# Column sums of the first FFN's modulation vectors: from matmuls against ones to trees of accumulating DMAs

## The chip, the cores and the metric

The kernel runs on one core of one Trainium2 chip. The metric is device time in microseconds. A core has five engines that matter here, each with its own instruction stream in a fixed order: TensorE (PE: matmuls; PEld is its weight load), VectorE (DVE), ScalarE (ACT), GpSimd (POOL) and SyncE (SP). SP here only issues DMAs; GpSimd can issue DMAs too. An engine starts its next instruction when the one before is done with it and the semaphores that it waits for have come. Matmul results land in PSUM, in banks of 128 partitions by 512 fp32 columns; all else lies in SBUF, with 128 partitions.

## The reference

Two layers over 256 latent tokens (and, in layer 0, 256 context tokens) of width 1024. Each layer is an FFN, a mixer (attention in layer 0, a short convolution in layer 1) and an FFN again. Every sub-layer is modulated by nine vectors, made from a conditioning vector:

```
m  = (silu(c)     @ ada_w[i] + ada_b[i]).reshape(BATCH, 9, 1, D)   # latent
mc = (silu(c_ctx) @ ada_w[i] + ada_b[i]).reshape(9, D)             # context
def half_step_ffn(x, shift, scale, gate, w_in, w_out, g, b):
    y = swiglu_ffn(x * (1 + scale) + shift, w_in, w_out)           # (silu(a) * u) @ w_out
    return layer_norm(DN_ALPHA * x + 0.5 * gate * y, g, b)
x   = half_step_ffn(x,   m[:, 0], m[:, 1], m[:, 2], ...)
ctx = half_step_ffn(ctx, mc[0],   mc[1],   mc[2],   ...)
hx, hc = x * (1 + m[:, 4]) + m[:, 3], ctx * (1 + mc[4]) + mc[3]    # into attention
```

`D` is 1024, the FFN's inner width 2816. `ada_w` is 1024 x 9216 per layer. The vectors are matrix-vector products: little arithmetic, much weight traffic, and a sum over all 1024 rows.

## The kernel before

**Matmuls and weight units.** A fp32 product is made from two halves: ScalarE copies a weight tile into a rounded high half (L216, for activations L118), VectorE subtracts it to make the low half (L219, L119), and TensorE adds up high x high, high x low and low x high. The step on VectorE is called a split here, L219 for weights. A weight unit is one load by SP (`w1r`, `w2r`, `wqr`), two high and two low pieces (`w1h`, `w1l` and so on). The raw tiles rotate through 4 buffers, the high and the low ones through 5 each (`WB`). In the first FFN every sixth unit takes its halves from one extra pair (`whx`, `wlx`, `ext[0] = 1`), so there are six in all.

**The first FFN** takes latent and context tokens together: four tiles of 128 tokens, 512 columns. It runs in three parts (`fh`), with 4, 4 and 3 panels of inner columns. In a part, TensorE multiplies the panels (`f`, L725), ScalarE and VectorE form silu(a)·u (VectorE's products are L735) and split it (`gh`, `gl`). Then the part's share of `w_out` follows, bank after bank: first half of the width (n = 0) for the four token tiles, then the second; each bank takes 24 matmuls in the first two parts. When a bank is done, VectorE does the residual: L415 multiplies it by the gate (`res`), L420 or L418 adds it to the token tile (`x`, `xc`). In the last part the layer norm follows: BN_STATS (L422), the aggregate (L429), two small operations on GpSimd for the standard deviation (`rs`, L431 and L432), the normalisation (L442), then transposes and modulated activations `hT` (ScalarE's high, VectorE's low half), and the attention's query product with four weight units (`wqr`, `wqh`, `wql`; TensorE's tile `wq`).

**The background stream** makes the modulation vectors of this stage beside the FFN. It is a generator, `ada`; the FFN's code calls `tick()` after each pair of matmul groups, and the stream goes one step further when its rate (0.45 and 0.44 steps per tick) has added up to one. A step loads 128 rows of one vector's columns (`ar`, 512 KB, SP, 3 buffers). VectorE multiplies them by the conditioning vector's entries and adds them into an accumulator of 128 partitions x 1024 (`acc`, 2 buffers): L302 for the first of eight loads, L304 multiply-add for the others, each in two halves of 512. After eight loads an accumulator is whole, but each partition still holds its own part of the sum. The seven groups of the stage, two vectors each, 14 in all:

```
set_background(stream([(0, 2, 0), (0, 2, 1)], [(0, 3, 0), (0, 3, 1)], [(0, 4, 0), (0, 4, 1)],
                      [(0, 5, 0), (0, 6, 0)], [(0, 7, 0), (0, 8, 0)], [(1, 0, 0), (1, 1, 0)],
                      [(1, 2, 0), (1, 3, 0)]), 0.45)
```

The triples are layer, vector, and 0 for latent or 1 for context. The first three groups share one weight load between the two vectors; the last four hold two different vectors, each of them loaded for itself. The first group is the gate of the first FFN itself, the second and third are shift and scale for attention.

**The end of a group.** Two fp32 matmuls per vector against a 128 x 32 tile of ones sum the partitions (L339, bank `ada`); VectorE adds the bias rows (`adab`, loaded by SP), and SP writes the result to `scr`, a DRAM tile with a row for each vector. From there it is read back where it is needed: the gate broadcast to all partitions (SP, L789, after the first part's panels), and shift and scale as rows for a transpose (`fold_cols`, tile `mrow`, L389) ahead of the last part's output product. Those 28 matmuls stand in TensorE's queue among the FFN's.

In later stages vectors are summed another way (`on_pool`): GpSimd's own reduction over the partitions (`red`, L353), and an accumulating DMA from GpSimd's queue into `scr` (L354).

**What sets the order.** TensorE's order is that of the code. On the other engines a scheduler orders instructions by priority and by when it reckons their operands are there; code in a `high_priority` block goes ahead or, with a negative offset, behind. A tile's buffers are reused in order: the first writer of a new tile waits for the last reader of the one that had the buffer.

Of the kernel before, what the change touches and what calls it, by code (L numbers as in the profile page):

```python
# [18 lines left out]
P = 128  # L19
D = 1024  # L20
# [55 lines left out]
def backbone_kernel(  # L76
# [20 lines left out]
    last_split, last_lo = [], []  # L97
    ext = [1, 0]
    ada_late = [0]
# [141 lines left out]
    win_sb = cp.tile([P, 64], F32, tag="wmask", name="wmask")  # L241
    ones = cp.tile([P, 32], F32, tag="ones", name="ones")
    ident = cp.tile([P, P], F32, tag="ident", name="ident")
# [22 lines left out]
    nc.scalar.activation(cst[:, :, 0:2], pt[:, 0:16].rearrange("p (v k) -> p k v", v=2), AF.Silu)  # L266
    nc.vector.memset(ones, 1.0)
    sel = cp.tile([P, 4], F32, tag="sel", name="sel")
# [9 lines left out]

    bias_rows = []
    on_pool = [False]  # L280
# [3 lines left out]
    def ada(vecs):  # L284
# [4 lines left out]
        def accumulate(l, m, k, w):  # L289
            with ExitStack() as st:  # L290
                for i in gate_ins + (last_lo if on_pool[0] else []):
                    st.enter_context(tc.issue_after(i.ins))
                for i, vec in enumerate(vecs):
                    if vec[:2] != (l, m):
                        continue
                    if k == 0:
                        acc[i] = hp.tile([P, D], F32, tag="acc", bufs=2, name=nm("acc"))
                    sc = cst[:, k, vec[2]:vec[2] + 1]
                    for h in range(2):
                        src, a = (c[:, h * 512:(h + 1) * 512] for c in (w, acc[i]))  # L300
                        if k == 0:
                            nc.vector.tensor_scalar(a, src, sc, None, op0=ALU.mult)  # L302
                        else:
                            nc.vector.scalar_tensor_tensor(out=a, in0=src, scalar=sc, in1=a,  # L304
                                                           op0=ALU.mult, op1=ALU.add)
            if on_pool[0] and k == KC - 1:
                sums.extend((vec, acc[i]) for i, vec in enumerate(vecs) if vec[:2] == (l, m))

# [13 lines left out]
        if on_pool[0]:  # L322
            return
        n = 2 * len(vecs)
        if not bias_rows:
            bias_rows.append(hp.tile([P, 512], F32, tag="adab", name=nm("adab")))
            nc.gpsimd.memset(bias_rows[0], 0.0)
        bt = bias_rows[0]
        for i, (l, m, v) in enumerate(vecs):
            sync.dma_start(bt[64 * i:64 * i + 64:32], ada_b[l, m * D:(m + 1) * D].rearrange("(a b) -> a b", b=512))  # L330
        yield 1
        yield 1
        yield 1
        rows = hp.tile([P, 512], F32, tag="adar", name=nm("adar"))
        ps = tpb("ada")
        for i in range(len(vecs)):
            for h in range(2):
                j = 2 * i + h
                nc.tensor.matmul(ps[32 * j:32 * j + 32, :], ones, acc[i][:, h * 512:(h + 1) * 512], start=True, stop=True)  # L339
# [43 lines left out]

    def fold_cols(l, v, m, ln):

        r = sm.tile([32, P], F32, tag="mrow", bufs=2, name=nm("mrow"))
        for i, src in enumerate((scr[l][v, (m + 1) * D:(m + 2) * D], scr[l][v, m * D:(m + 1) * D],
                                 ln_g[ln[0], ln[1]], ln_b[ln[0], ln[1]])):
            sync.dma_start(r[8 * i:8 * i + 8], src.rearrange("(a b) -> a b", b=P))  # L389

# [202 lines left out]
    w_in, w_out = ffn_w_in[0, 0], ffn_w_out[0, 0]  # L593
    ab0 = hp.tile([P, D], F32, tag="acc", bufs=2, name="ab0")
    nc.vector.memset(ab0, 0.0)
# [151 lines left out]
    for q, (k0, n) in enumerate(steps):  # L747
        nxt = start_step(*steps[q + 1]) if q < 4 else iter(())
        for g in range(6 * n):
# [21 lines left out]
    for fh, (p0, p1) in enumerate(parts):  # L771
# [517 lines left out]
```

## Time and profile before

| what | value |
|---|---|
| time, median of 3 runs | 1247.95 us (1247.05 to 1248.7) |
| the profiled execution | 1247.93 us |
| its span in the profile | 1246.1 us |
| granted TensorE clock, mean | 0.999 |
| memory traffic | 275.67 MB, mean 221 GB/s |
| GpSimd's DMA queue (q0) | 160 packets, 0.02 MB |

How to read the profile: the busy share says how much of the span an engine worked. The chain follows the work that ended last back to what released it at each step, and says by whose work the end was set. The windows cut the span in stretches; the stage of the change runs to about 412 us. In timeline rows the columns are start in us from the span's start, duration in us, engine, line, operation and tiles (out<-in) and how many instructions the row joins; brackets give the wait ahead of it and what ended it. `PEclk` is the granted clock of TensorE. A name such as `ar<-in_ada_w_dram` is a DMA from a DRAM input into the tile `ar`.

### The profile page before, as it was taken

Reading aid. Unit: us, or ns where it says so; the run is one execution under the profiler, and the core shown is the slowest. Engines: PE = TensorE matmul, PEld = TensorE weight load, DVE = VectorE, ACT = ScalarE, POOL = GpSimd, SP = SyncE. Lnnn points to the kernel's source line nnn. Section 1 sums busy time; section 2 is a strip of 40 time slices with the busy share of each in tenths; the row PEclk is TensorE's granted clock in tenths of the full one; section 3 lists DMA queues with packets and bytes.
Section 4 is the critical chain, followed back from the end, with each engine's and each line's share of the span. In section 5 each row is a group of like instructions: output and inputs, shape, how many; then the busy total and the mean of one; then the engine's idle time right before and its main releaser. Section 6 shows DMA issues by size and latency. Waiting matters only on the chain.

```text
span 1246.1 us, 17225 instructions
## 1 busy us (share of the span) xinstructions
PE 1227.6 (99%) x5794; PEld 994.6 (80%) x5794; DVE 964.0 (77%) x1675; ACT 644.7 (52%) x1233; POOL 81.7 (7%) x90
## 2 busy tenths in 40 slices
PE   8999999999999999999999999999999999999997
PEld 5787778778778878777888888888878877888886
DVE  3698987788868867888877677878768798877646
ACT  2433132322325556587778635668635644677631
POOL 0000000000001011120000020020020110000200
PEclk9999999999999999999999999999999999999999
DMA  9976678778852654455899857889956764899741
GB/s 308 309 246 213 190 236 287 260 266 274 286 179 79 183 118 87 114 109 145 261 303 299 276 200 248 230 255 317 300 198 221 219 219 153 224 302 257 252 156 68
DMA packets 232304, 275.67 MB, mean 221 GB/s; under 512 B 59622, under 2 KB 178910, under 8 KB 232216
## 3 DMA queue, kind: packets, MB, share of 16 engines
q1 hardware_dynamic: 232020, 274.54, 73.0%
q8 instruction: 45, 0.74, 0.2%
q14 instruction: 43, 0.35, 0.1%
q0 software_dynamic: 160, 0.02, 0.1%
q10 hardware_dynamic: 36, 0.02, 0.0%
HBM read 265.27 MB, written 2.20 MB: 215 GB/s over the span
## 4 chain that ended last, share of the span: by engine, by line
PE 87%; DVE 4%; DMA 4%; ACT 2%; issue 2%; SPq 1%; POOL 0%; DVEq 0%; ACTq 0%
PE f L725 19%; PE w L170 17%; PE w L171 17%; PE w L173 17%; PE wkv L170 2%; PE wkv L171 2%; PE wkv L173 2%; DMA ar<-in_ada_w_dram 2%; PE wc L170 1%; PE wc L173 1%; PE wc L171 1%; DMA wor<-in_na_w_out_dram 1%; PE S L1020 1%; PE hT L450 1%; DMA wcr<-in_sc_w_in_dram 1%
## 5 line engine op out<-in xcount | busy, mean ns | idle before, releaser
L219 DVE TENSOR_TENSOR w1l<-w1r,w1h 128x512 fp32r<-128x512 f32 (+1 forms) x352 | 230.4, 698 | 44.2 <-ACT w1h L216 43.3
L216 ACT ACTIVATE w1h<-w1r 128x512 fp32r<-128x512 f32 (+1 forms) x352 | 198.4, 618 | 115.5 <-PE w L173 52.8
L170 PE MATMUL w<-w1h,hTh 128*128 128x512 f32 x528 | 206.2, 391 | 1.3 <-ACT hTh L118 1.3
L171 PE MATMUL w<-w1l,hTh 128*128 128x512 f32 x528 | 205.6, 389 | 0.0
L304 DVE SCALAR_TENSOR_TENSOR acc<-ar,cst,acc 128x512 f32<-128x512 f32 x266 | 186.6, 746 | 10.8 <-DMA ar<-in_ada_w_dram 10.8
L170 PE MATMUL w<-w2h,gh 128*128 128x512 f32 (+1 forms) x446 | 173.4, 389 | 0.0
L171 PE MATMUL w<-w2l,gh 128*128 128x512 f32 (+1 forms) x446 | 172.3, 387 | 1.1 <-DVE w2l L219 1.1
L216 ACT ACTIVATE w2h<-w2r 128x512 fp32r<-128x512 f32 x176 | 101.5, 624 | 135.0 <-PE w L173 102.9
L173 PE MATMUL w<-w1h,hTl 128*128 128x512 f32 x528 | 162.6, 389 | 0.0
L219 DVE TENSOR_TENSOR w2l<-w2r,w2h 128x512 fp32r<-128x512 f32 x176 | 113.9, 687 | 54.7 <-ACT w2h L216 53.3
L173 PE MATMUL w<-w2h,gl 128*128 128x512 f32 (+1 forms) x446 | 136.1, 386 | 0.0
L725 PE MATMUL f<-h0h,w1h 128*128 128x512 f32 x352 | 132.8, 393 | 1.2 <-ACT w1h L216 0.6
L725 PE MATMUL f<-h0l,w1h 128*128 128x512 f32 x352 | 133.2, 391 | 0.0
L725 PE MATMUL f<-h0h,w1l 128*128 128x512 f32 x352 | 132.7, 390 | 0.0
L170 PEld LDWEIGHTS w<-w1h,hTh 128*128 128x128 f32 x528 | 99.1, 188 | 22.5 <-ACT hTh L118 2.1
L173 PEld LDWEIGHTS w<-w1h,hTl 128*128 128x128 f32 x528 | 99.0, 188 | 21.0 <-DVE hTl L119 0.4
L171 PEld LDWEIGHTS w<-w1l,hTh 128*128 128x128 f32 x528 | 99.1, 188 | 20.6 <-DVE w1l L219 0.3
L170 PEld LDWEIGHTS w<-w2h,gh 128*128 128x128 f32 x446 | 83.8, 188 | 19.2 <-issue 1.7
L171 PEld LDWEIGHTS w<-w2l,gh 128*128 128x128 f32 x446 | 83.8, 188 | 18.3 <-DVE w2l L219 1.9
L173 PEld LDWEIGHTS w<-w2h,gl 128*128 128x128 f32 x446 | 83.3, 188 | 17.1
L725 PEld LDWEIGHTS f<-h0h,w1h 128*128 128x128 f32 x352 | 65.5, 188 | 19.6 <-issue 4.2
L725 PEld LDWEIGHTS f<-h0l,w1h 128*128 128x128 f32 x352 | 65.5, 188 | 14.4 <-issue 1.0
(195 smaller groups left out, 1765.8 us busy)
## 6 DMA issues: line engine op xcount, KB each, us to landing
w1r<-in_ffn_w_in_dram SPq DMA_DIRECT2D x340, 256.0 KB
ar<-in_ada_w_dram SPq DMA_DIRECT2D x128, 512.0 KB
w2r<-in_ffn_w_out_dram SPq DMA_DIRECT2D x88, 512.0 KB
ar<-in_ada_w_dram SPq DMA_DIRECT2D x32, 256.0 KB
wkvr<-in_na_w_qkv_dram SPq DMA_DIRECT2D x32, 256.0 KB
wcr<-in_sc_w_in_dram SPq DMA_DIRECT2D x32, 256.0 KB
wqr<-in_na_w_qkv_dram SPq DMA_DIRECT2D x8, 512.0 KB
wor<-in_na_w_out_dram SPq DMA_DIRECT2D x8, 512.0 KB
```

Of the source, the lines that this page charges most:

```text
L170: nc.tensor.matmul(ps, lh, rh, start=first and i == 0, stop=False)
L171: nc.tensor.matmul(ps, lh, rl, start=False, stop=False)
L173: nc.tensor.matmul(ps, ll, rh, start=False, stop=last and i == n - 1)
L216: last_split[:] = [nc.scalar.activation(hi[:, a:a + m // W_HI], raw[:, a:a + m // W_HI], AF.Copy)]
L219: last_lo[:] = [nc.vector.tensor_tensor(out=lo[:, a:b], in0=raw[:, a:b], in1=hi[:, a:b].bitcast(F32), op=ALU.subtract)]
L304: nc.vector.scalar_tensor_tensor(out=a, in0=src, scalar=sc, in1=a, op0=ALU.mult, op1=ALU.add)
L450: nc.tensor.transpose(ps[:, k * P:(k + 1) * P], z[h][:, k * P:(k + 1) * P], ident)
L725: nc.tensor.matmul(ps, w, hT0[k][part == 1], start=(k == part == 0), stop=(k == KC - 1 and part == 1))
L1020: nc.tensor.matmul(banks[i], (qh, qh, ql)[f][ps, qs], (kh, kl, kh)[f][ps, :], start=f == 0, stop=f == 2)
```

## The change

The ones, the bias rows, the matmuls, their eviction and SP's writes are gone. When a group's last load is accumulated, a tree halves the accumulator seven times: the DMA adds partitions n to 2n-1 onto 0 to n-1, for n = 64, 32, ... 1. An eighth accumulating DMA adds row 0 to the vector's row in `scr`, into which three DMAs from SP have put the biases ahead of the stage. All tree steps are on GpSimd's queue, as are now the gate's broadcast and the `scr` rows of `mrow`. Each step needs the one before it on the same accumulator. The accumulators are five instead of two; the extra pair of weight halves is given up for them (`ext[0] = 0`). Where the group ended with four steps of the stream, five empty ones stand now.

```diff
-    ext = [1, 0]
+    ext = [0, 0]
...
-                        acc[i] = hp.tile([P, D], F32, tag="acc", bufs=2, name=nm("acc"))
+                        acc[i] = hp.tile([P, D], F32, tag="acc", bufs=2 if on_pool[0] else 5, name=nm("acc"))
...
-            if on_pool[0] and k == KC - 1:
-                sums.extend((vec, acc[i]) for i, vec in enumerate(vecs) if vec[:2] == (l, m))
+            if k == KC - 1:
+                ready = [(vec, acc[i]) for i, vec in enumerate(vecs) if vec[:2] == (l, m)]
+                if on_pool[0]:
+                    sums.extend(ready)
+                    return
+                n = P // 2
+                while n:
+                    for _, a in ready:
+                        nc.gpsimd.dma_start(a[0:n], a[n:2 * n], accum_op=ALU.add)
+                    n //= 2
+                for (l, m, v), a in ready:
+                    nc.gpsimd.dma_start(scr[l][v:v + 1, m * D:(m + 1) * D], a[0:1], accum_op=ALU.add)
...
-        for i, (l, m, v) in enumerate(vecs):
-            sync.dma_start(bt[64 * i:64 * i + 64:32], ada_b[l, m * D:(m + 1) * D].rearrange("(a b) -> a b", b=512))
-        yield 1
-        yield 1
-        yield 1
-        rows = hp.tile([P, 512], F32, tag="adar", name=nm("adar"))
-        ps = tpb("ada")
-        for i in range(len(vecs)):
-            for h in range(2):
-                j = 2 * i + h
-                nc.tensor.matmul(ps[32 * j:32 * j + 32, :], ones, acc[i][:, h * 512:(h + 1) * 512], start=True, stop=True)
-        nc.vector.tensor_tensor(out=rows[:32 * n], in0=ps[:32 * n], in1=bt[:32 * n], op=ALU.add)
-        for i, (l, m, v) in enumerate(vecs):
-            sync.dma_start(scr[l][v, m * D:(m + 1) * D].rearrange("(a b) -> a b", b=512),
-                           rows[64 * i:64 * i + 64:32, :])
-        yield 1
+        for _ in range(5):
+            yield 1
...
-    def fold_cols(l, v, m, ln):
+    def fold_cols(l, v, m, ln, q=sync):
...
-            sync.dma_start(r[8 * i:8 * i + 8], src.rearrange("(a b) -> a b", b=P))
+            (q if i < 2 else sync).dma_start(r[8 * i:8 * i + 8], src.rearrange("(a b) -> a b", b=P))
...
+    for l, v, r in ((0, 0, slice(2 * D, 9 * D)), (0, 1, slice(2 * D, 5 * D)), (1, 0, slice(0, 9 * D))):
+        sync.dma_start(scr[l][v, r].rearrange("(a b) -> a b", a=16), ada_b[l, r].rearrange("(a b) -> a b", a=16))
     sync.dma_start(win_sb, win_mask)
...
-                sync.dma_start(big.rearrange("p a b -> p (a b)"),
+                nc.gpsimd.dma_start(big.rearrange("p a b -> p (a b)"),
...
-            GB = [fold_cols(0, v, 3, (0, 0)) for v in range(2)]
+            GB = [fold_cols(0, v, 3, (0, 0), nc.gpsimd) for v in range(2)]
...
-    sync.dma_start(scr[1][0, 4 * D:9 * D].rearrange("(a b) -> a b", a=16), ada_b[1, 4 * D:9 * D].rearrange("(a b) -> a b", a=16))
```

Three places show how the order moves; a row joins like instructions (x2), and the numbers behind the tiles' names count the tiles. In the changed kernel lines are numbered anew: L713 is the FFN's matmul that was L725, L403 the residual that was L415, L301 the multiply-add that was L304, L419 GpSimd's part of the layer norm that was L431.

**TensorE, third panel of the first part.** Before, the first group's ones matmuls stand between two weight units of the panel (`w1h_867`, then `w1h_876`):

```order
L725 MATMUL f_160_951<-h0h_449,w1l_868 128x512
L725 MATMUL f_160_951<-h0l_450,w1h_867 128x512
L339 MATMUL ada_971<-acc_711,ones 32x512 x2
L339 MATMUL ada_971<-acc_714,ones 32x512 x2
L725 MATMUL f_160_951<-h0h_545,w1h_876 128x512
L725 MATMUL f_160_951<-h0h_545,w1l_877 128x512
```

Now:

```order
L713 MATMUL f_159_964<-h0l_426,w1h_868 128x512
L713 MATMUL f_159_964<-h0h_447,w1h_868 128x512
L713 MATMUL f_159_964<-h0h_447,w1l_869 128x512
L713 MATMUL f_159_964<-h0l_448,w1h_868 128x512
L713 MATMUL f_159_964<-h0h_543,w1h_877 128x512
```

The two rows of L339 are gone and the unit's matmuls follow each other; at the other six places it is the same, and nothing else moves on TensorE.

**VectorE, the first residuals of the first part.** Before, the residual of the first token tile stands among the multiply-adds of the second group (`acc_994`, `acc_997`), ahead of the first split of the next `w_out` unit (`w2l_1311`):

```order
L304 SCALAR_TENSOR_TENSOR acc_994<-ar_1177,cst,acc_994 128x512
L415 SCALAR_TENSOR_TENSOR res_1197<-w_190_1136,gate_1124 128x512
L304 SCALAR_TENSOR_TENSOR acc_994<-ar_1177,cst,acc_994 128x512
L420 SCALAR_TENSOR_TENSOR x_122<-x_122,res_1197 128x512
L304 SCALAR_TENSOR_TENSOR acc_997<-ar_1177,cst,acc_997 128x512 x2
L304 SCALAR_TENSOR_TENSOR acc_994<-ar_1207,cst,acc_994 128x512 x2
L304 SCALAR_TENSOR_TENSOR acc_997<-ar_1207,cst,acc_997 128x512 x2
L415 SCALAR_TENSOR_TENSOR res_1233<-w_203_1200,gate_1124 128x512
L219 TENSOR_TENSOR w2l_1311<-w2r_1309,w2h_1310 128x512
L420 SCALAR_TENSOR_TENSOR x_124<-x_124,res_1233 128x512
L219 TENSOR_TENSOR w2l_1311<-w2r_1309,w2h_1310 128x512
L219 TENSOR_TENSOR w2l_1326<-w2r_1324,w2h_1325 128x512 x2
```

Now:

```order
L219 TENSOR_TENSOR w2l_1312<-w2r_1310,w2h_1311 128x512
L403 SCALAR_TENSOR_TENSOR res_1195<-w_186_1134,gate_1122 128x512
L219 TENSOR_TENSOR w2l_1312<-w2r_1310,w2h_1311 128x512
L408 SCALAR_TENSOR_TENSOR x_120<-x_120,res_1195 128x512
L299 TENSOR_SCALAR acc_1379<-ar_1377,cst 128x512 x2
L299 TENSOR_SCALAR acc_1382<-ar_1377,cst 128x512 x2
L301 SCALAR_TENSOR_TENSOR acc_1379<-ar_1397,cst,acc_1379 128x512 x2
L301 SCALAR_TENSOR_TENSOR acc_1382<-ar_1397,cst,acc_1382 128x512
L403 SCALAR_TENSOR_TENSOR res_1251<-w_199_1198,gate_1122 128x512
L301 SCALAR_TENSOR_TENSOR acc_1382<-ar_1397,cst,acc_1382 128x512
L408 SCALAR_TENSOR_TENSOR x_122<-x_122,res_1251 128x512
L301 SCALAR_TENSOR_TENSOR acc_1379<-ar_1425,cst,acc_1379 128x512 x2
```

The second group is through before the first residual, half a split stands ahead of it, and behind it come the third group's products (L299) and multiply-adds (L301): four and eleven of them stand between the first residual and the split of `w2l_1327`, the unit that follows, with two more residuals.

**GpSimd, from its first DMA, and ahead of the layer norm.** Before, no DMA of this stage is on GpSimd's queue: behind the set-up its next instruction is the layer norm's `rs`. Now the first group's tree and the gate stand first; these are the pair's last halving, the eighth step, the gate, and the start of the second group's tree:

```order
L311 DMA acc_712<-acc_712 1x16x64
L311 DMA acc_715<-acc_715 1x16x64
L314 DMA scr_114<-acc_712 16x1x64
L314 DMA scr_114<-acc_715 16x1x64
L779 DMA gate_1122<-scr_114 128x1024
L779 DMA gate_1124<-scr_114 128x1024
L311 DMA acc_1016<-acc_1016 64x1024
L311 DMA acc_1019<-acc_1019 64x1024
```

The stage's last tree and the layer norm's first operations:

```order
L311 DMA acc_3097<-acc_3097 16x1024
L311 DMA acc_3097<-acc_3097 8x1024
L311 DMA acc_3097<-acc_3097 4x1024
L311 DMA acc_3097<-acc_3097 2x1024
L311 DMA acc_3097<-acc_3097 1x16x64
L314 DMA scr_115<-acc_3097 16x1x64
L419 TENSOR_TENSOR rs_3379<-mv_3377,lnc 128x1
L420 TENSOR_TENSOR rs_3379<-rs_3379,lnc 128x1
```

Two accumulators alternate level by level in the first three groups; in the others each vector has a tree of its own, and the layer norm stands behind all 14.

More of the change, by code (lines that the diff above doesn't have):

```diff
@@ L241, in backbone_kernel @@
     win_sb = cp.tile([P, 64], F32, tag="wmask", name="wmask")
-    ones = cp.tile([P, 32], F32, tag="ones", name="ones")
     ident = cp.tile([P, P], F32, tag="ident", name="ident")
@@ L266, in backbone_kernel @@
     nc.scalar.activation(cst[:, :, 0:2], pt[:, 0:16].rearrange("p (v k) -> p k v", v=2), AF.Silu)
-    nc.vector.memset(ones, 1.0)
     sel = cp.tile([P, 4], F32, tag="sel", name="sel")
@@ L276, in backbone_kernel @@
     xscr = tc.dram_tile([2 * P, D], F32, name="xscr")
-    bias_rows = []
     on_pool = [False]
@@ L593, in backbone_kernel @@
     w_in, w_out = ffn_w_in[0, 0], ffn_w_out[0, 0]
-    ab0 = hp.tile([P, D], F32, tag="acc", bufs=2, name="ab0")
+    ab0 = hp.tile([P, D], F32, tag="acc", bufs=2 if on_pool[0] else 5, name="ab0")
     nc.vector.memset(ab0, 0.0)
```

5 lines of the change are left out of this document (removed).

## The prediction

> **What bounds the kernel now.** I read the page first: busy times, then the chain.
>
> ```profile
> span 1246.1 us, 17225 instructions
> PE 1227.6 (99%) x5794; PEld 994.6 (80%) x5794; DVE 964.0 (77%) x1675; ACT 644.7 (52%) x1233; POOL 81.7 (7%) x90
> PE 87%; DVE 4%; DMA 4%; ACT 2%; issue 2%; SPq 1%; POOL 0%; DVEq 0%; ACTq 0%
> ```
>
> TensorE is busy 99% of the span, and 87% of the chain that ended last is its own work. The table by windows shows the stage of the change:
>
> ```profile
> core 0: us, PE busy (x) PEld busy (x) DVE busy (x) ACT busy (x) POOL busy (x), PEclk, DMA share, GB/s
> 50.00:100.00 50.00, 50.00 (x225) 40.47 (x224) 43.28 (x73) 18.38 (x33) 0.00 (x0) 1.00 0.73 232
> 100.00:150.00 50.00, 50.00 (x225) 40.47 (x224) 47.75 (x77) 13.34 (x23) 0.00 (x0) 1.00 0.71 222
> 300.00:350.00 50.00, 50.00 (x225) 40.47 (x224) 41.00 (x65) 14.22 (x25) 0.00 (x0) 1.00 0.86 278
> 350.00:412.00 62.00, 62.00 (x294) 50.47 (x293) 48.23 (x91) 31.01 (x67) 3.33 (x8) 1.00 0.35 104
> ```
>
> In the first FFN, up to 412 us, TensorE never stops and its granted clock is 1.00 (the windows between read the same). So whatever leaves its queue there shortens the run, if nothing else makes it wait. VectorE is the near rival: 47.75 of 50 us between 100 and 150. GpSimd is idle until 350.
>
> **Term 1: the column sums leave TensorE.** Seven groups end in fp32 matmuls against a column of ones; the chain has them as seven pieces, first and last:
>
> ```profile
> 96.56 1.00 PE ada L339 x8
> ...
> 360.95 1.00 PE ada L339 x8
> ```
>
> A piece costs more than its 1.00, because the stream of FFN matmuls breaks and restarts. TensorE's timeline around the third piece:
>
> ```profile
> 171.83 0.39 PE L725 MATMUL f<-h0h,w1l 128*128 128x512 f32 x1
> 172.06 0.39 PE L725 MATMUL f<-h0l,w1h 128*128 128x512 f32 x1
> 172.38 1.06 PE L339 MATMUL ada<-acc,ones 128*32 128x512 f32 x8
> 173.38 0.50 PE L725 MATMUL f<-h0h,w1h 128*128 128x512 f32 x1
> ...
> 174.64 0.40 PE L725 MATMUL f<-h0l,w1h 128*128 128x512 f32 x1
> ```
>
> The FFN matmul that starts at 174.64 is the sixth behind the one at 172.06 (four lie in the gap). Undisturbed they start 0.227 us apart (171.83 to 172.06), six in 1.36; the rest of the 2.58 us, 1.22, is the piece. Seven of them: **-8.5 us** (by the chain's own 1.00 it would be -7.0, the small end of this term).
>
> VectorE also loses seven evictions of about 0.6 us, and SP some 30 small transfers. Neither is the bound, so I count nothing. A wait goes with them:
>
> ```profile
> DVE acc L302 <- PE ada L339: 6.1, 3, 2.9
> ```
>
> It cost nothing while TensorE was full. But without it, and with five accumulators, VectorE takes the multiply-adds earlier, as term 4 uses.
>
> **Term 2: when does the first gate arrive?** A tree is a chain on GpSimd: seven halvings, an accumulate into DRAM, then the gate's broadcast, each waiting for the one before. The trace of before has no SBUF-to-SBUF accumulate. The nearest rows are the five accumulates into DRAM late in the run, one of them with what VectorE did then and with SP's read that waited for it:
>
> ```profile
> L354 POOL DMA_DIRECT2D scr<-red x5: 997/997/1118, 727.3 to 1158.5; - x5
> DMA to landing us min/median/max: 2.6/3.5/4.0
> 912.27 1.28 DVE L219 TENSOR_TENSOR w2l<-w2r,w2h 128x512 fp32r<-128x512 f32 x2
> 913.01 1.00 POOL L354 DMA_DIRECT2D scr<-red  x1 [0.29 <-POOL red L353]
> 916.37 0.30 SPq L389 DMA_DIRECT2D mrow<-scr  x1
> ```
>
> From issue to the dependent issue is 913.01 to 916.37, 3.4 us; over the five a hop is 2.6 to 4.0, 1.0 of it the issue. Two accumulators per level issue in 2.0, less than a hop, so a pair costs one chain. These rows move 4 KB. The first two levels move 256 and 128 KB, and the gate 512 KB; loads of 256, 512 and 256 KB stand in the chain:
>
> ```profile
> 22.81 5.03 DMA ar<-in_ada_w_dram
> 558.60 11.95 DMA wor<-in_na_w_out_dram
> 1043.05 2.93 DMA w1r<-in_ffn_w_in_dram
> ```
>
> I take 4.5 and 4.0 for the two wide levels (estimates, between 2.93 and 5.03), 3.5 for the other six hops, and 5.0 for the gate, near the 5.03: 4.5 + 4.0 + 6 x 3.5 + 5.0 = 34.5. Where the tree starts, and who waits:
>
> ```profile
> 84.85 2.73 DVE L304 SCALAR_TENSOR_TENSOR acc<-ar,cst,acc 128x512 f32<-128x512 f32 x4
> 98.61 1.27 DVE L302 TENSOR_SCALAR acc<-ar,cst 128x512 f32<-128x512 f32 x3
> 120.94 0.69 DVE L415 SCALAR_TENSOR_TENSOR res<-w,gate 128x512 f32<-128x512 f32 x1
> 122.81 4.06 DVE L304 SCALAR_TENSOR_TENSOR acc<-ar,cst,acc 128x512 f32<-128x512 f32 x6
> ```
>
> The first group was whole at 87.6; in the new order one split that waits for a buffer (five pairs, not six) stands ahead, so 88.5. The gate lands at 88.5 + 34.5 = **123.0**. Its first reader, the residual, ran at 120.9; the new order brings VectorE there at about 120. VectorE works in order, so a late gate holds all behind it, up to the split of the next weight unit that TensorE needs: eleven multiply-adds at 0.66 (4.06 for six), four products at 0.40, seven instructions of 0.60 (1.28 for two splits above), 13.1 in all, then the split, 1.2. TensorE fills a bank in 24 matmuls, 5.44 us, so it began the half at 115.5 and ends it four banks and one piece later, at 138.4; two pieces gone make that 136.0. The second unit's second low part is wanted nine matmuls, 2.0 us, later, at 138.0: a gate at 123.7 would just do. The fourth unit's is wanted 21 matmuls on, at 140.8, with seven more instructions of 0.60 ahead of its end: **123.4**, the latest harmless gate. So **no stall**, by 0.4 us; a margin of 11 by the low ends (8 x 2.6 + 2.9 lands at 112.2), a stall of 9 by the high ends (8 x 4.0 + 12 lands at 132.5).
>
> The row at 912.27 matters once more: VectorE read two SBUF operands right through the issue at 913.01, and it stayed at 1.00 us. The Trainium skill (SBUF — State Buffer, section "SBUF: two separate sides") speaks against the change: GpSimd writes its DMA descriptors through a port pair that VectorE can lock, and a transfer of 620 ns took 3100 beside a copy in a two-port mode. No row of this case shows such a delay; it is part of a rival below. The other way, the skill (DMA: Bandwidth & Descriptors, section "Anatomy of one DMA — SWDGE (gpsimd) path") fits 2.0 us plus the bytes at 436 GB/s; an estimate by that page lands the gate near 109, without a stall. The rows of 2.6 to 4.0 are above it.
>
> **Term 3: the handover to the query weights.** With five buffers the third and fourth query units are split late, among the last layer norms:
>
> ```profile
> 402.07 0.23 PE wq L170
> 401.79 0.20 DVE L429 BATCH_NORM_AGGREGATE mv<-st 128x2 f32<-128x12 f32 x1
> 403.26 1.00 DVE L442 TENSOR_SCALAR xc<-xc,mv,rs 128x512 f32<-128x512 f32 x2 [0.71 <-POOL rs L432]
> 385.26 0.21 DVE L429 BATCH_NORM_AGGREGATE mv<-st 128x2 f32<-128x12 f32 x1
> ```
>
> On the old clock the aggregate comes at 400.7 in the new order (two splits that stood ahead are gone), the normalisation waits 1.3 for GpSimd as before (401.9 to 403.3), takes 1.0, and the fourth unit's second half follows at 403.0 to 403.6. TensorE starts that unit at 402.07 and wants the half three matmuls on, at 402.75: **+0.9** (nothing if the scheduler's two swap in time, 2.5 if the third unit is late too). At the other handovers the same sums leave 2.7 to 3.5 us, so nothing.
>
> **Term 4: cover that could go.** GpSimd's queue holds 112 tree steps ahead of the layer norm's small operations. From these rows I date the sums:
>
> ```profile
> 171.20 0.69 DVE L735 TENSOR_TENSOR sil<-sil,f 128x512 f32<-128x512 f32 x1 [0.26 <-PE f L725]
> 317.50 0.68 DVE L735 TENSOR_TENSOR sil<-sil,f 128x512 f32<-128x512 f32 x1
> 351.69 0.74 DVE L304 SCALAR_TENSOR_TENSOR acc<-ar,cst,acc 128x512 f32<-128x512 f32 x1
> ```
>
> In the new order the first lone vector is whole five multiply-adds behind the product of 171.20, about 176; the last, which ended at 351.69, stands behind the product of 317.50, less six pieces: about 313. That is one per 19.5 us. A lone tree needs five hops and an issue of the queue (its first level overlaps the end of the tree before): 18.5 at 3.5. So the queue keeps up and is through by 340. The layer norm asks at 385.26 - 8.5 = 376.8; the queue is late only if 176 + 42 hops + 9 issues exceeds that, at hops above **4.6**. Nothing is added.
>
> **Sum.** The profiled execution took 1247.93, 1.8 more than its span and level with the median of 1247.95: 1247.93 - 8.5 + 0 + 0.9 = **1240.3**.
>
> **Rivals.**
> - Gate late: hops at 4, or the gate load near 12. Stall 2 to 11 us, 1242.5 to 1251.5. For it: VectorE has no room to catch up. Against: the median of 3.5. Chance 0.13.
> - Slower than before: hops above 4.6, because wide levels are slow among the loads (0.10) or VectorE starves the descriptors, the rule above (0.06). At 5: gate at 133.5, stall 10.1; the queue frees at 395 where the delayed layer norm asks at 386.9, 8.1 more: 1239.4 + 0.9 + 18.2 = 1258.5. The sign turns at a stall of 7.6, a mean hop of 4.7. Chance 0.16.
> - The DMA engines fill: their share was 0.86 at 300, and 14 trees move 127 rows of 4 KB each, read twice, among weights. Five handovers lose 1 or 2 us each beyond their slack: 1243 to 1252. Chance 0.08.
> - The change doesn't give: the 8.5 us come back in the attention stage, whose chain has the load of 11.95 us: 1247. Against: such loads start when buffers come free, which moves along. Chance 0.06.
>
> **How the numbers follow.** The forecast holds 0.57, from 1238.6 (no handover loss, and 0.8 for the spread of the runs) to 1243. The range goes up to 1252, which takes in the gate's high ends and leaves out most of the slow hops, some 0.15 with the bottom edge. Faster by over 0.2% (2.5 us, about what a measurement of this kernel tells from no change): 0.57, half of the late gate, part of the third rival, 0.67. Within: 0.16. Slower: 0.17, nearly all slow hops.
>
> **What would show it.** Right: no matmul against ones, the gate landing near 123, hops of 3 to 4.5 us, TensorE without a gap around 138 and with one near 1 us before 400. Wrong: a residual that waits long for the gate's transfer, the layer norm's GpSimd operations late behind trees, multiply-adds that wait for their loads while splits queue behind them.

## The result: slower by 3.6%

| kernel | time | ratio to before |
|---|---|---|
| before | 1247.96 (1247.05 to 1248.7) | |
| the change | 1295.82, median of 4; 1292.53, median of the three used for the ratio | 1.0358, 95% interval 1.0335 to 1.0382 |
| forecast | 1240.3 (1238.6 to 1252.0) | 0.994 |

Three of the change's runs took 1285.55 to 1299.11 us; the fourth took 2485.69, for which nothing here has an explanation, and the ratio leaves it out. The profiled run took 1292.53, and comparisons below use this number, 44.6 over before.

### The profile after

From the page, the span, the busy times, the chain and GpSimd's DMA queue (packets, MB, share):

```profile
span 1290.7 us, 17222 instructions
PE 1236.4 (96%) x5738; PEld 1001.7 (78%) x5738; DVE 958.4 (74%) x1667; ACT 645.1 (50%) x1233; POOL 173.5 (13%) x207
PE 60%; DMA 23%; DVE 9%; issue 3%; ACT 2%; POOL 1%; SPq 1%; DVEq 0%; POOLq 0%; ACTq 0%
q0 software_dynamic: 5056, 8.44, 4.1%
```

TensorE was 87% of the chain; now it is 60%, and DMAs are 23%, 16 of it tree steps by the page's list of lines. The table by windows, for the first FFN:

```profile
100.00:150.00 50.00, 42.28 (x179) 33.98 (x178) 40.75 (x66) 13.40 (x23) 17.48 (x23) 0.93 0.79 221
150.00:200.00 50.00, 45.90 (x191) 37.38 (x190) 39.26 (x64) 10.72 (x19) 16.06 (x21) 0.94 0.85 251
200.00:250.00 50.00, 45.33 (x189) 36.59 (x187) 35.04 (x56) 13.43 (x24) 14.95 (x20) 0.95 0.93 281
250.00:300.00 50.00, 44.46 (x182) 34.96 (x183) 37.97 (x61) 10.20 (x18) 11.82 (x15) 0.97 0.91 281
300.00:350.00 50.00, 45.94 (x189) 36.93 (x188) 40.85 (x66) 10.31 (x19) 10.55 (x13) 0.93 0.91 280
350.00:400.00 50.00, 48.81 (x215) 39.97 (x215) 24.57 (x39) 17.32 (x30) 14.19 (x18) 1.00 0.52 139
```

Before, TensorE was busy for all 50 us of each at clock 1.00. Now, up to 350, it idles 4 to 8 us in each, and its mean clock is 0.93 to 0.97; in the last row it idles 1.2 at clock 1.00. VectorE did not take its place as the bound: it is busy for less of each window than before as well (40.75 us where it was 47.75 in the first). The waits say for whom, first TensorE's, then VectorE's, and last VectorE's wait for loads before (total us, times, longest):

```profile
PE f L713 <- DVE w1l L219: 14.7, 5, 4.1
PE w L171 <- DVE w2l L219: 10.1, 3, 6.6
PE w L170 <- ACT gh L118: 1.9, 2, 1.0
...
DVE acc L301 <- DMA ar<-in_ada_w_dram: 44.6, 28, 4.4
DVE sil L723 <- PE f L713: 11.4, 2, 7.9
DVE res L403 <- DMA gate<-scr: 8.6, 1, 8.6
...
DVE acc L304 <- DMA ar<-in_ada_w_dram: 10.8, 18, 1.9
```

TensorE waits for low halves of weights, and VectorE, which makes them, stands in multiply-adds that wait for their loads (44.6 us; 10.8 before) and once in the residual that waits for the gate. The windows around TensorE's longest wait show what a wait costs besides:

```profile
140.00:144.00 4.00, 0.79 (x4) 0.32 (x2) 4.00 (x7) 0.85 (x2) 0.66 (x1) 0.91 0.78 197
144.00:148.00 4.00, 0.66 (x2) 0.56 (x3) 4.00 (x8) 0.00 (x0) 0.87 (x2) 0.50 0.66 166
148.00:152.00 4.00, 4.00 (x11) 3.13 (x10) 4.00 (x7) 0.00 (x0) 1.62 (x2) 0.50 0.68 174
152.00:156.00 4.00, 4.00 (x15) 3.17 (x15) 4.00 (x8) 0.00 (x0) 1.61 (x2) 0.81 1.00 307
156.00:160.00 4.00, 4.00 (x19) 3.30 (x19) 4.00 (x7) 0.00 (x0) 0.79 (x1) 1.00 0.89 309
```

The clock falls to 0.50 while TensorE still waits, and behind the gap it does 11 matmuls in the 4 us where it does 19 at full clock.

**The sum of the loss.** The first query matmul (`wq`) starts at 431.6 where it started at 396.9, +34.7, by these rows before and after:

```profile
L170 PE MATMUL wq<-wqh,hTh x32: 389/395/499, 396.9 to 506.3; 128*128 128x512 f32 x32
...
L170 PE MATMUL wq<-wqh,hTh x32: 388/391/500, 431.6 to 544.9; 128*128 128x512 f32 x32
```

Of that the pieces give -8.1 (below), TensorE's waits up to there 27.2 (14.7 + 10.1 + 1.9 and 0.5 smaller), the slow clock 14.0 (the clock's shortfall in the five windows from 100 to 350, times 50). But 2.8 of the 14.0 lie inside the waits, as in the window from 144 to 148, and count once: together 30.3. Of the 4.4 left over, some 2 are the overlap of neighbouring matmuls, lost at each of 13 waits (an estimate: a matmul takes 0.39 and the next starts 0.227 after it); the rest is open. Attention adds 4.0 (the last `wkv` matmul is 38.7 later than before). The span's end adds 5.9, to 44.6: SyncE's last issue ends at 1281.7, 9.0 before the end; before, at 1243.3, 2.8 before it.

### The profile page after: what moved, and what is told of

It is laid out like the page before. It is cut to its first block, busy times and chain, and to the rows that moved or that the text cites. A ratio compares the mean times of both kernels' runs of the same rounds, so it can differ in the third digit from the quotient of the medians.

```text
span 1290.7 us, 17222 instructions
## 1 busy us (share of the span) xinstructions
PE 1236.4 (96%) x5738; PEld 1001.7 (78%) x5738; DVE 958.4 (74%) x1667; ACT 645.1 (50%) x1233; POOL 173.5 (13%) x207
## 4 chain that ended last, share of the span: by engine, by line
PE 60%; DMA 23%; DVE 9%; issue 3%; ACT 2%; POOL 1%; SPq 1%; DVEq 0%; POOLq 0%; ACTq 0%
DMA acc<-acc 16%; PE w L170 14%; PE w L171 14%; PE w L173 14%; DMA ar<-in_ada_w_dram 3%; PE f L713 3%; PE wkv L170 2%; PE wkv L171 2%; PE wkv L173 2%; DVE acc L301 1%; PE wc L170 1%; PE wc L171 1%; PE wc L173 1%; DVE w1l L219 1%; DMA wor<-in_na_w_out_dram 1%
## 5 line engine op out<-in xcount | busy, mean ns | idle before, releaser
L301 DVE SCALAR_TENSOR_TENSOR acc<-ar,cst,acc 128x512 f32<-128x512 f32 x266 | 186.2, 750 | 44.7 <-DMA ar<-in_ada_w_dram 44.6
L713 PE MATMUL f<-h0h,w1l 128*128 128x512 f32 x352 | 136.5, 401 | 14.7 <-DVE w1l L219 14.7
L713 PE MATMUL f<-h0h,w1h 128*128 128x512 f32 x352 | 135.8, 402 | 0.4 <-DVE h0h L668 0.4
L713 PE MATMUL f<-h0l,w1h 128*128 128x512 f32 x352 | 135.8, 399 | 0.0
L311 POOL DMA_DIRECT2D acc<-acc x98 | 78.7, 843 | 304.5 <-DMA acc<-acc 215.9
L173 PEld LDWEIGHTS w<-w2h,gl 128*128 128x128 f32 x446 | 83.9, 189 | 18.5 <-DVE gl L119 1.3
L713 PEld LDWEIGHTS f<-h0h,w1l 128*128 128x128 f32 x352 | 67.8, 193 | 31.3 <-DVE w1l L219 17.1
```

The source lines that it names most:

```text
L173: nc.tensor.matmul(ps, ll, rh, start=False, stop=last and i == n - 1)
L311: nc.gpsimd.dma_start(a[0:n], a[n:2 * n], accum_op=ALU.add)
L713: nc.tensor.matmul(ps, w, hT0[k][part == 1], start=(k == part == 0), stop=(k == KC - 1 and part == 1))
```

## The experiments

Three theories on the FFN's loss stood at the start: **gate** (the late gate and its wake), **DMA** (the trees' traffic delays the loads) and **order** (VectorE's new order and the missing pair of weight halves). All runs were compared with the kernel before on the same chip; its medians there were 1246.85 to 1248.02.

| run | us | ratio to before (95%) |
|---|---|---|
| e1 gate free | 1287.26 | 1.0318 (1.0294 to 1.0343) |
| e2 no halvings | 1260.48 | 1.0108 (1.0083 to 1.0133) |
| e3 thin halvings | 1287.11 | 1.0311 (1.0294 to 1.0327) |
| e4 before, 4 accumulators, no pair | 1258.10 | 1.0083 (1.0066 to 1.0100) |
| e5 before, no pair | 1253.54 | 1.0048 (1.0033 to 1.0062) |
| e6 no halvings, pair, 2 accumulators | 1255.74 | 1.0078 (1.0061 to 1.0096) |
| e7 trees, pair, 3 accumulators | 1313.55 | 1.0530 (1.0516 to 1.0544) |
| e8 late groups by GpSimd's reduction | 1279.26 | 1.0247 (1.0231 to 1.0263) |
| e9 = e6, paced | 1247.60 | 1.0002 (0.9991 to 1.0014) |
| e10 = change, paced | 1311.17 | 1.0509 (1.0496 to 1.0523) |
| e11 = before, paced | 1247.82 | 1.0002 (0.9993 to 1.0011) |
| e12 = e9 + three narrow halvings | 1247.25 | 1.0000 (0.9984 to 1.0016) |
| e13 = e10, one tree per group | 1260.96 | 1.0101 (1.0084 to 1.0118) |
| e14 = e13, gate free | 1251.10 | 1.0025 (1.0011 to 1.0039) |
| e15 = e13, not paced | 1295.04 | 1.0376 (1.0355 to 1.0397) |

### Taking the parts out: e1 to e4

e1 reads the gate from `ada_b`, with nothing to wait for:

```diff
-                nc.gpsimd.dma_start(big..., bass.AP(scr[0].tensor, scr[0][v, 2 * D:3 * D].offset, [[0, P], [1, D]]))
+                sync.dma_start(big..., bass.AP(ada_b.tensor, ada_b[0, 2 * D:3 * D].offset, [[0, P], [1, D]]))
```

> The changed kernel, but the first FFN's gate is read from the bias rows in DRAM, on SyncE's queue, and not from the tree's result (so the gate lacks the product with the weights: that part of the computation is left out). All trees stay. VectorE's order is the same row for row. Theory 'gate': the late gate (VectorE waited 8.6 us for it, TensorE then 6.6, at half the granted clock behind it) starts the loss, and the later stalls are its wake: 1245 to 1258. Theory 'DMA': the trees' transfers among the loads make the loads late, whatever the gate does: the stall at 140 goes (6.6 and some 4 of slow clock), the five waits for low halves between 190 and 360 stay: 1275 to 1285. Theory 'order': VectorE's new order with the pair of weight halves gone is the cause: also 1275 to 1285.

e2 starts the loop with `n = 0`, which leaves the accumulate into DRAM alone:

> The changed kernel without the seven halvings of every tree; only the last step, row 0 into DRAM, is left (the sums over the other 127 partitions are left out). VectorE's order is the same but for one multiply-add. Theory 'gate' and theory 'DMA' both: all that was lost is back and the seven pieces of TensorE are gained, 1238 to 1243. Theory 'order': the gate is early, but VectorE still stands behind loads of ada_w while splits wait: 1255 to 1285.

e3 keeps every hop but 64 columns wide, `a[0:n, 0:64]` from `a[n:2 * n, 0:64]`:

> The changed kernel with the same 98 halvings, each over 64 columns of the accumulator and not 1024 (the sums of the other 960 columns are left out): as many hops and partitions, a sixteenth of the bytes; the gate's 512 KB read stays. Theory 'bytes': a hop is 2 to 3 us, the gate lands by 118, 1238 to 1246. Theory 'queueing': a hop's time is that of small packets behind the loads on the same DMA engines, whatever its size: hops of 4 us, the gate lands at 123 to 128, and the time lies between, 1245 to 1275.

e4 is the kernel before with `ext = [0, 0]` and four accumulators:

> The kernel before, with the ones matmuls, but without the extra pair of weight halves and with four accumulators in place of two (five do not fit beside the bias and result rows): the buffers of the change without its trees. Theory 'order': VectorE runs into waits for ada_w and splits come late, 1260 or more. Theories 'gate' and 'DMA': little, 1246 to 1253.

No theory holds alone. Freeing the gate saved 5.3 us of 44.6 (e1, a little over the range of DMA and order), and as three runs of the change lie 13.6 apart that is hardly clear of noise. Without any halving the kernel was still 12.8 slower than before (e2), in the range of order. Most of the change's buffers without its trees (no pair, four accumulators) cost 10.4 (e4), between the two ranges. And a sixteenth of the bytes (e3), 27 us over e2, was outside both ranges of that run. The waits of e3 show something new:

```profile
PE hT L438 <- DVE x L430: 11.8, 1, 11.8
...
DVE x L430 <- POOL rs L420: 15.1, 2, 14.2
```

With the FFN less delayed, the layer norm waited 14.2 us for GpSimd's small operation `rs`, which stood in the queue behind the last trees. In the change itself that wait does not show:

```profile
396.78 1.07 POOL L314 DMA_DIRECT2D scr<-acc  x1
401.62 0.75 POOL L311 DMA_DIRECT2D acc<-acc  x1 [3.77 <-DMA acc<-acc]
...
419.04 0.76 POOL L314 DMA_DIRECT2D scr<-acc  x1 [3.38 <-DMA acc<-acc]
420.31 0.19 POOL L419 TENSOR_TENSOR rs<-mv,lnc 128x1 f32<-128x1 f32 x1 [0.51 <-DVE mv L417]
```

Its queue is through at 419.8, half a microsecond before the delayed layer norm asks. From the first step at 89.9 to there, GpSimd waits for little but its own DMAs: 216 us for hops of `acc` in the view of its waits, 17 for the last hops of trees and 4 for all else. So a second limit lay close behind the first.

### The pair and VectorE's order: e5, e6, e9, e11

e5 is the kernel before with `ext = [0, 0]` and nothing else; e6 is e2 with the pair back and two accumulators, which is the kernel before without the ones matmuls.

> The kernel before without the extra pair of weight halves, all else as it was (two accumulators, ones matmuls). e4, with four accumulators besides, cost 10.4 us. Theory 'pair': the missing pair makes splits late in the first FFN and again in attention, 1255 to 1259, with the 1.7 us wait for kTl and the 1.3 us wait for wql that all runs without the pair had. Theory 'running ahead': the accumulators beyond two let VectorE run into loads of ada_w, and the pair costs 0 to 3: 1248 to 1251.

> The changed kernel without halvings (the sums over 127 partitions are left out, as in e2), with the extra pair back and two accumulators: the kernel before without its ones matmuls, their eviction and small transfers. It prices term 1 alone. By the prediction 8.5 us less than before, 1239 to 1241; by the chain's own 1.00 a piece, 1240.5 to 1242; if the gain is given back later in attention, 1245 to 1248.

e5 lies between the theories, at +6.7: 1.9 by the first `wq` matmul (398.8), 7.0 by the last `wkv` one (548.2). The pair is worth some 5 us in attention, where the prediction had not looked. e6 was the surprise: the seven pieces gone, no tree, the pair there, and 8.9 us **slower** than before. VectorE's timeline in e6, ahead of a wait of TensorE:

```profile
249.63 1.42 DVE L301 SCALAR_TENSOR_TENSOR acc<-ar,cst,acc 128x512 f32<-128x512 f32 x2 [0.27 <-DMA ar<-in_ada_w_dram]
252.13 1.42 DVE L301 SCALAR_TENSOR_TENSOR acc<-ar,cst,acc 128x512 f32<-128x512 f32 x2 [1.09 <-DMA ar<-in_ada_w_dram]
253.77 2.08 DVE L301 SCALAR_TENSOR_TENSOR acc<-ar,cst,acc 128x512 f32<-128x512 f32 x3 [0.22 <-DMA ar<-in_ada_w_dram]
255.76 2.50 DVE L219 TENSOR_TENSOR w2l<-w2r,w2h 128x512 fp32r<-128x512 f32 x4
```

TensorE waited 2.67 us for the `w2l` that starts at 255.76, behind multiply-adds whose data trickled in. Before, an accumulator came free only when its ones matmuls had run. The order that was made around that wait of VectorE (6.1 us, which the prediction dropped as costless) spread the multiply-adds over 81 stretches between other work, where e6 has 53. e9 paces them by another tie, which the later stages have already:

```diff
-                for i in gate_ins + (last_lo if on_pool[0] else []):
+                for i in gate_ins + last_lo:
                     st.enter_context(tc.issue_after(i.ins))
```

> e6 (no halvings, pair back, two accumulators; the sums over 127 partitions are left out) with one edit: every accumulation is put behind the last weight split ahead of it in the code, as the later stages do. On VectorE the multiply-adds and their waits for ada_w then stand in 74 stretches and not 53 (81 in the kernel before). e6 took 1255.74. Theory 'running ahead' (without the ones matmuls' wait, VectorE's static order puts bursts of multiply-adds ahead of splits and stands in them waiting for loads, TensorE waits and restarts at half clock): 1239 to 1245. Theory 'bound' (the stage cannot go faster than VectorE and the loads, whatever the order): 1247 to 1256.

> The kernel before with the same edit as e9, as a control (79 stretches on VectorE, 81 without it): both theories 1245 to 1251, since its accumulators already pace VectorE.

e9 took 0.1 us more than before where e6 took 8.9 more, though it did not reach the 1239 to 1245 expected: of its profile's waits 4.6 us at the ends of the FFN's parts are left, for ScalarE's `gh`, and the longer one, 3.2, restarts at half clock. The control e11 did not move. So running ahead is shown; why the gain of the pieces stays out in the median is only partly shown.

e12's profiled run, at 1242.14 the fastest of its ten (1242.14 to 1254.9), prices the pieces: `wq` starts at 391.3, 5.6 earlier than before, with one wait of 2.5 on the way, thus **8.1** for the seven. This is one profile against one, good to about 1 us: e12's first FFN matmul starts at 12.1 where it started at 11.0, so by the FFN's own length the pieces are worth 9.3.

### Two limits, each enough: e10, e13, e14, e15

e10 is the change with that edit.

> The changed kernel, complete, with the same edit as e9 (63 stretches on VectorE, 55 without it). Theory 'running ahead' predicts that some 10 us come back, 1280 to 1287: the gate's hops, the trees' bytes among the loads, the 6 us at the program's end and the missing pair stay. Theory 'bound': 1290 to 1300.

It became slower by some 19 us, against both theories, and its profile says why. TensorE was busy for all 50 us of each window from 150 to 350, at clock 1.00: these stalls of the FFN were gone, with the trees' traffic there. One of these windows, and then two rows of VectorE's timeline:

```profile
200.00:250.00 50.00, 50.00 (x222) 41.42 (x221) 41.12 (x66) 17.46 (x30) 12.63 (x17) 1.00 0.93 307
...
385.21 0.21 DVE L417 BATCH_NORM_AGGREGATE mv<-st 128x2 f32<-128x12 f32 x1
438.17 1.00 DVE L430 TENSOR_SCALAR x<-x,mv,rs 128x512 f32<-128x512 f32 x2 [52.75 <-POOL rs L420]
```

The layer norm asked at 385.4 and got its `rs` at 438: 52.75 us behind trees. e13 shortens the queue at the same bytes, with the accumulators of a group in one tile. There are two such tiles, so four accumulators where the change has five, and a tree starts when both are whole:

```diff
-                    for _, a in ready:
-                        nc.gpsimd.dma_start(a[0:n], a[n:2 * n], accum_op=ALU.add)
+                    nc.gpsimd.dma_start(both[0][0:n], both[0][n:2 * n], accum_op=ALU.add)
```

> e10 (complete, paced) with the two accumulators of a group in one tile and one tree for both: a halving is one DMA over 2048 columns, and GpSimd's queue holds 49 halvings and not 98, the same bytes. Nothing is left out. In e10 the layer norm's GpSimd operation stood 52 us behind trees. Theory 'queue' (the serial chain of hops on GpSimd's queue sets when the layer norm can go on): that wait falls below 10, and what is left over the 1247.5 of before is the gate (7 to 10), the missing pair (5), 1 to 3 at the program's end, less 8.5 of pieces: 1252 to 1266. Rival 'bytes': hops over twice the columns last twice as long, the queue is no shorter: 1285 or more.

> e13 with the gate read from the bias rows as in e1 (the gate lacks its product with the weights). It takes the late gate out of e13: if the parts add up, 1245 to 1254 (1247.5 - 8.5 + 5 for the pair + 1 to 3 at the end + up to 5 of waits at the ends of the FFN's parts), and 7 to 10 below e13. If the gate hides behind something else, e13 and e14 agree within 3.

> e13 without the pacing edit: the change as it was, but with one tree per group. Theory 'queue' with 'running ahead': the floor that the queue sets is gone and the stalls by bursts of multiply-adds (e2 took 1260.5 without any halving) and the gate are left: 1265 to 1278, between e13 and the change. If the change's loss was the queue alone, as e13; if it was the bursts alone, 1290 as the change.

| | as scheduled | paced |
|---|---|---|
| a tree per vector | 1292.5 (the change) | 1311.2 (e10) |
| a tree per group | 1295.0 (e15) | 1261.0 (e13) |

Either edit alone gives nothing or costs; both together give 32 us. VectorE's bursts delay the FFN by about as much as the queue delays the layer norm, so taking one away uncovers the other. e13 fell into its range. e15 lay above its 1265 to 1278 and near the case that its expectation gave to the bursts alone, but not by bursts alone:

```profile
PE w L171 <- DVE w2l L219: 15.7, 4, 9.4
...
DVE acc L304 <- DMA scr<-acc: 14.3, 2, 12.4
```

TensorE's longest wait there, 9.4 us up to 155.3, follows one of VectorE, 12.4 up to 139.2, for an accumulator that a tree still held, and one of 4.8 for the gate. With five accumulators this first wait might not be there, so how much the shorter queue gains alone is not known to some us; e13, which is paced, has no such wait. In e13 the layer norm waits 1.0 us for `rs` at most, as before. e14 takes the gate's wait for the tree out of e13: -9.9, as its theory had it. What is left of e14 over before is 3.1 us.

### Other ways that did not work: e7, e8, e12

> The changed kernel, trees and all, with the extra pair back and three accumulators (all that fits then). Theory 'pair': some 20 us of the loss go (e2 kept 12.5 us over before without any tree, and 8.5 of gain lay under it), 1268 to 1278. Rival: a tree holds its accumulator for 30 us or more, so with three of them VectorE waits for buffers in place of loads, and the time is as long or longer: 1285 to 1310.

e7 went past its rival's range: VectorE waited 33.9 us for accumulators that trees still held, besides 33.2 for loads.

e8 sums the last four groups by `partition_all_reduce` in place:

```diff
+                for (l, m, v), a in ready:
+                    nc.gpsimd.partition_all_reduce(a, a, P, ReduceOp.add)
+                    nc.gpsimd.dma_start(scr[l][v:v + 1, m * D:(m + 1) * D], a[0:1], accum_op=ALU.add)
```

> The kernel before, where the last four groups (eight vectors, one every 19.5 us) are summed by GpSimd's own reduction over the partitions, in place in the accumulator, and one accumulating DMA into scr each; biases ahead in scr; the first three groups, pair and accumulators as before. Four pieces of TensorE go, 4 x 1.22 = 4.9 us. If the reduction (6.1 us in the profile of before) and some 7 us ahead of it fit into 19.5 us and VectorE does not slow beside it: 1242 to 1244, faster than both kernels. Rival: accumulators come back late (13 and a hop of 3.5, plus VectorE's static order) or VectorE's instructions lengthen beside the reduction, and TensorE waits for splits: 1248 to 1260.

It was slower than its rival's range, by the second cause that the rival names. VectorE's groups from 200 to 350 us, in e8 and then before (busy us, mean ns):

```profile
L303 DVE TENSOR_SCALAR acc<-ar,cst 128x512 f32<-128x512 f32 x12 | 25.0, 2119 | 1.4 <-DMA ar<-in_ada_w_dram 1.4
L219 DVE TENSOR_TENSOR w2l<-w2r,w2h 128x512 fp32r<-128x512 f32 x16 | 14.5, 951 | 0.0
...
L302 DVE TENSOR_SCALAR acc<-ar,cst 128x512 f32<-128x512 f32 x12 | 5.4, 481 | 5.0 <-PE ada L339 2.9 <-DMA ar<-in_ada_w_dram 2.1
L219 DVE TENSOR_TENSOR w2l<-w2r,w2h 128x512 fp32r<-128x512 f32 x18 | 11.6, 685 | 0.7 <-ACT w2h L216 0.7
```

The means hide two cases. Of the twelve products in e8, four that began beside a reduction took 3.8 to 4.8 us and the four right behind them 1.1 to 1.7; the other four took 0.47 to 0.48. Of the sixteen splits one, beside a reduction, took 5.03, and the others 0.67 to 0.69.

> e9 with the last three halvings of each tree (8 rows to 1), 42 DMAs more on GpSimd's queue and little traffic (the sums over 120 partitions are left out). For the time between SyncE's last issue and the end of the span, 2.8 us in the kernel before and in e2 (25 GpSimd DMAs), 9.0 in every run with whole trees (123 or so). Theory 'count': it grows with the DMAs on that queue, about 0.06 us for each above some number, so 4 to 6 us here. Theory 'kind': it belongs to accumulates from SBUF to SBUF as such: 9. Rival: it starts only above some number of DMAs: 2.8. In all else 2 to 8 us over e9, by two accumulators held three hops longer.

For the program's end, e12 fits the count: 67 GpSimd DMAs, 4.4 us from SyncE's last issue to the end (2.8 with 5 and with 25 DMAs, 5.0 with e13's 74, 9.0 with the 123 of the change). The short hops cost nothing else, against the 2 to 8 us expected: its median is e9's.

No version beat the kernel before. The nearest complete one with trees is e13, 13 us over it.

## Why the prediction was wrong, step by step

Two steps failed, and either is enough for most of the loss: term 3 put the waits at the FFN's handovers at nothing, and term 4 let the queue keep up.

- **Term 1, the pieces: right.** -8.5 forecast, -8.1 by e12's profile, to about 1 us.
- **Term 2, the gate: right in form, mis-sized.** It was to land at 123.0; VectorE's residual started on it at 133.5. The tree began at 89.9 (88.5 forecast), the two wide levels took 8.1 and 6.0 us (4.5 and 4.0), the six others 24.6 (21.0), the gate's read 4.9 (5.0):

```profile
89.92 1.15 POOL L311 DMA_DIRECT2D acc<-acc  x1 [88.31 <-DVE acc L301]
97.97 0.81 POOL L311 DMA_DIRECT2D acc<-acc  x1 [5.91 <-DMA acc<-acc]
104.01 0.78 POOL L311 DMA_DIRECT2D acc<-acc  x1 [2.95 <-DMA acc<-acc]
128.65 1.26 POOL L779 DMA_DIRECT2D gate<-scr  x2 [1.48 <-PE w L173]
133.51 0.69 DVE L403 SCALAR_TENSOR_TENSOR res<-w,gate 128x512 f32<-128x512 f32 x1 [8.63 <-DMA gate<-scr]
```

  (The profile names a matmul for the gate's 1.48; by the code its issue also needs the accumulates into `scr` just ahead.) By the prediction's own limit of 123.4 that is a stall of 10.1, and e13 less e14 measured 9.9. That the two agree is in part luck: TensorE waited only 6.6 us in the change and 6.3 in e13, and the rest is the half clock behind it, which the prediction did not have.
- **Term 3, the handovers: the step that failed first.** The query weights cost 1.3 us (0.9 forecast). But "at the other handovers the same sums leave 2.7 to 3.5 us, so nothing" reckoned with VectorE's work and not with its waits: in the new order bursts of multiply-adds stand ahead of splits and wait for their loads, 44.6 us where it was 10.8. The prediction names this among its signs of being wrong and counts nothing for it in the sum. e2, e6 and e9 show it, and e13 against e15 gives its size, 34 us with the trees' traffic beside it and e15's wait for an accumulator in it. And the sixth pair was looked at up to the FFN's end only: e5 shows 5 us in attention.
- **Term 4, the queue: the step that hid the size.** "18.5 at 3.5. So the queue keeps up and is through by 340": it was through at 419.8. In the stretch from 241.5 to 351.5 a lone vector's tree came every 27.5 us (four intervals between the accumulates into DRAM), a hop of 5.3 by the prediction's count of five hops and an issue. When the loads had ended (DMA share 0.52 from 350 to 400), the last two came after 18.6 and 22.3, near the forecast. The five rows that gave 3.5 had been taken at DMA shares of 0.25 to 0.59; the first FFN runs at 0.8 to 0.9. With hops 64 columns wide (e3) the two first levels fell from 7.8 and 5.2 to 4.6 and 4.0 (medians from issue to landing), the five others only from between 3.4 and 4.5 to between 2.8 and 3.9. So the bytes lengthen the wide levels; that the rest is waiting beside the loads fits the shares, and was not tested by itself.
- **Not in the sum at all:** the half clock behind five of TensorE's waits, 14.0 us with the 2.8 inside them, and the end of the program, 6 us.
- **The rivals.** "Slower: hops above 4.6" with the queue late for the layer norm was the right mechanism, with a chance of 0.16; at 5 it was priced 1258.5. That this is near the 1261.0 of e13 is luck: e13 has the late gate, but neither bursts nor a late queue. The DMA engines filling, with a chance of 0.08, is not what held TensorE: in e10 it never stopped from 150 to 350 at a DMA share of 0.91 to 0.93. That VectorE would starve GpSimd's descriptors (the rule of the Trainium skill, SBUF — State Buffer, section "SBUF: two separate sides") does not show in the issues: GpSimd's 98 halvings took 0.79 us each to issue at the median, 1.54 at most, beside a VectorE that was busy 70 to 80% of the time. Whether some of it lies in the time to landing was not tested. The Trainium skill's other figure for such a DMA (DMA: Bandwidth & Descriptors, section "Anatomy of one DMA — SWDGE (gpsimd) path"), 2.0 us plus the bytes, which would be 2.6 for the first level, was a third of the 7.8 measured among loads.

## What to carry to other kernels

A wait that costs nothing can be what paces an engine that works in order: before taking it away, ask which instructions will run ahead into waits of their own, and what stands behind them. Price a hop of a dependent DMA chain at the DMA share of the stage where it will run, and multiply it over the whole queue up to the next operation that others need, not only up to the first consumer. When two limits are of one size, undoing either shows nothing; cross the two edits.

## What the runs showed of the hardware that was not expected

- A wait of TensorE of 2.3 us was enough for half clock in e6: it waits up to 121.85, and the windows from 122 on read 0.51 and 0.63, with 1.00 from 126. The Trainium skill (TensorE: Matmul & The Clock Gate, section "Part 1: The HAM clock gate (the "warmup" mystery)") puts the fall at an idle window of about 3.4 us; the half clock behind e6's wait lasted 3.4 us (matmuls 0.43 apart from 121.85 to 125.4), the gap before it was shorter. The length of the wait alone does not decide: one of 3.01 us in the change (up to 277.92) and one of 2.67 in e6 (up to 256.50) left the clock at 1.00, and one of 2.04 in e6 (up to 328.94) was followed by half clock. In the clock records of a trace the half-clock stretches of the first FFN begin whole multiples of 3.41 us apart (143.26, 197.87, 225.18, 252.48 and 327.58 in the change). Cut into stretches of 3.41 on that grid, the first FFN of all the kept traces has 39 at full clock in which TensorE idled 1.93 us or more, and all were followed by half clock; none of the 49 with 0.8 to 1.78 was. The 3.01 lay across a border, with no more than 1.61 idle in either stretch. (Behind the FFN one of 1.61, in e5, was followed by half clock, so the border is known for this stage only.)
- The end of the program lengthens with the number of GpSimd's DMAs: by 1.6 us at 67 and 6.2 at 123 of them, some 0.08 us for each between, and by nothing at 25. Their bytes do not matter: e3 has 123 too, with narrow halvings, and the same 9.0 us.
- GpSimd's reduction over the partitions holds up VectorE: a product with one SBUF operand that began beside one took 3.8 to 4.8 us in place of 0.48, which agrees with the exclusive lock that the Trainium skill's page SBUF — State Buffer describes in the section named above. GpSimd's accumulating DMAs do not slow it: the multiply-adds took 0.750 us in the change and 0.746 before.
